# Three modulation vectors: sums over the k tiles elementwise on VectorE, only the sum over partitions on TensorE

## The chip, the cores and the metric

The kernel runs on one core of one Trainium2 chip. The metric is the device time of one execution in microseconds (us). The time before is the median of three runs.

## What is computed

One layer of a hybrid network over 640 tokens (128 of a context, 512 latent ones) of width 1024, all in float32: a SwiGLU block (FFN1), a mixer of two branches (a delta rule and windowed attention), a second SwiGLU block (FFN2) and a last norm. Nine modulation vectors of width 1024 scale, shift and gate these blocks, each for two conditions (the context's and the latents'). They come from one product of a vector with a 1024 x 9216 matrix, and this product is what the change is about:

```python
mod_p = (jax.nn.silu(c_ctx) @ ada_w[l] + ada_b[l])[None, None, :]
mod_s = (jax.nn.silu(c) @ ada_w[l] + ada_b[l])[:, None, :]
sh1p, sc1p, g1p, sh2p, sc2p, g2p, sh3p, sc3p, g3p = jnp.split(mod_p, N_MOD, axis=-1)
...
xp = ffn_sublayer(xp, norm_ffn1[l], sh1p, sc1p, g1p, ffn1_w13[l], ffn1_w2[l])
...
xp = ffn_sublayer(xp, norm_ffn2[l], sh3p, sc3p, g3p, ffn2_w13[l], ffn2_w2[l])
```

Vectors 0 and 1 are needed before FFN1 starts, 2 at its first residual, 3 to 5 in the mixer, and 6 to 8 (sh3, sc3, g3) in FFN2.

## The kernel before

The program is written as one stream and each engine keeps its own queue, in the order that a scheduler gave the instructions at build time. A queue is worked off in order: an instruction that waits holds up all behind it.

FFN1 (`ffn`, lines 480 to 528) goes through the 22 column blocks f of the hidden width in six rounds (ROUNDS: f = 0 to 2, 3 to 6, 7 to 10, 11 to 13, 14 to 17, 18 to 21). In a round it first makes the gated hidden blocks, then multiplies them by w2 and adds the result to the residual x (the w2 round: 8 column blocks d, `gated_add`, line 455). For f < 3 the two products are made directly; from f = 3 on `product_pair` (lines 570 to 613) makes both with seven products of a quarter size, whose weights are first combined on POOL (lines 580 to 583, tiles `ss`). Every weight tile is split into a high and a low part, the high part on ScalarE (line 127, tiles `wh` and `sh`) and the rest on DVE (line 128, `wl` and `sl`), and each product is three matmuls. `nraw` = 3 buffers hold raw weights, `nsh` = 6 hold each of `sh` and `sl` in FFN1; a pair uses five. FFN2 is the same code with `nsh` = 5 and without modulation.

Modulation vectors 2 to 8 are made in between (`modulation`, lines 266 to 301, called through `between` of line 1525). A vector takes four steps. A step loads two raw tiles of 128 x 1024 (line 273, tiles `araw`, a ring of two buffers) and multiplies each on TensorE by the 32 columns wide stationary tile `s32` (line 277): four matmuls for a raw tile, one for each 256 columns, each into its own 32 partitions of a PSUM tile, so that they sit on four column groups of the array. Both tiles of a step add up in PSUM; DVE adds the step's result to `modr` (lines 286 and 288). After the fourth step two transposes (line 292) and one addition (line 293) bring the vector into place. `between` does one step after each f (two for f = 0 and 1), and one each after d = 3 and d = 7 of each w2 round but the last. Tiles of PSUM are the ring `aux` of four and `big` of two.

Line numbers are those of the kernel before; behind line 265 those of the kernel after are higher by 4 to 51.

Of the kernel before, what the change touches and what calls it, by code (L numbers as in the profile page):

```python
# [10 lines left out]
F32 = mybir.dt.float32  # L11
# [4 lines left out]
ALU = mybir.AluOpType  # L16
# [3 lines left out]
P = 128  # L20
D = 1024
# [77 lines left out]
class Net:  # L99
# [147 lines left out]
    def vectors(self):  # L247
        nc = self.nc
        c = self.const
        ps = self.aux_tile()  # L250
        nc.tensor.transpose(ps[:, 0:16], self.crows, self.ident[0:16, 0:16])
        sT = self.tile(c, [P, 16], F32, "sT")
        nc.scalar.activation(sT, ps[:, 0:16], AF.Silu)
        self.s32 = self.tile(c, [P, KD, 32], F32, "s32")
        for v in range(2):
            nc.vector.tensor_copy(
                self.s32.rearrange("p k (r v) -> p v k r", v=2)[:, v],
                sT[:, v * 8 : v * 8 + 8].unsqueeze(2).to_broadcast([P, KD, 16]),
            )
        ps = self.aux_tile()  # L260
        nc.tensor.transpose(ps[:, 0:105], self.vrows[0:105], self.ident[0:105, 0:105])
        self.vecT = self.tile(c, [P, 105], F32, "vecT")
        nc.vector.tensor_copy(self.vecT, ps[:, 0:105])
        self.mod = self.tile(c, [P, 9, KD, 2], F32, "mod")

    def modulation(self, m):


        nc, a = self.nc, self.a
        r = self.tile(self.small, [P, 256], F32, "modr", 2)  # L270
        for k in range(KD):
            raw = self.tile(self.apool, [P, D], F32, "araw", 2)
            nc.sync.dma_start(raw, a["ada_w"][0, k * P : (k + 1) * P, m * D : (m + 1) * D])
            if k % 2 == 0:
                ps = self.aux_tile()[:, 0:256]
            for g in range(4):
                nc.tensor.matmul(  # L277
                    ps[32 * g : 32 * g + 32],
                    lhsT=self.s32[:, k, :],
                    rhs=raw[:, g * 256 : (g + 1) * 256],  # L280
                    start=(k % 2 == 0),
                    stop=(k % 2 == 1),
                )
            if k % 2:
                if k == 1:
                    nc.vector.tensor_copy(r, ps)
                else:
                    nc.vector.tensor_tensor(r, r, ps, op=ALU.add)
                yield
        p2 = self.aux_tile()  # L290
        for h in range(2):
            nc.tensor.transpose(p2[:, h * P : (h + 1) * P], r[:, h * P : (h + 1) * P], self.ident)
        nc.vector.tensor_tensor(
            self.mod[:, m].rearrange("p (g h) v -> p g h v", h=2),
            p2[:, 0:256].rearrange("p (h g r) -> p g h r", h=2, g=4)[:, :, :, 0:2],
            self.vecT[:, m * 8 : m * 8 + 8]
            .rearrange("p (g h) -> p g h", h=2)
            .unsqueeze(3)
            .to_broadcast([P, 4, 2, 2]),
            op=ALU.add,  # L300
        )

    def modulation_part(self, m0, d0, nd):

# [1121 lines left out]
    def build(self):  # L1426
        nc, a, tc = self.nc, self.a, self.tc
# [10 lines left out]
        with (  # L1438
# [9 lines left out]
            with (  # L1448
                pool("x1") as xpool,
            ):  # L1450
                self.setup()
                xall = self.tile(xpool, [P, KD, 2, HT], F32, "x")
                X = [xall[:, d] for d in range(KD)]
                self.apool = xpool
                ss = self.tile(self.const, [P, NCH], F32, "ss1")
                with pool("ada0", side="right") as ada, ExitStack() as inner:
                    with pool("in1", side="right") as self.phase:
                        self.load_input(xall, ss)
                        r = self.token_rstd(ss)
                        self.vectors()  # L1460
                    self.phase = ada
                    A1 = self.tile(self.const, [P, KD, 2], F32, "A1")
                    hs = self.operand_tiles(KD)
                    rb = []
                    for cuts in (((0, 0, P), (1, 0, P), (2, 0, HD)), ((2, HD, HD), (3, 0, P), (4, 0, P))):
                        o, columns = 0, []
                        for t, t0, n in cuts:
                            columns.append((r[:, t : t + 1], t0, n, o))
                            o += n
                        rb.append(self.half_rows(columns))  # L1470
                    xp = inner.enter_context(pool("xn", side="right"))
                    xn = [self.tile(xp, [P, 2, HT], F32, "xn", KD) for _ in range(KD)]

                    def scaled(d):
                        for h in range(2):
                            nc.vector.tensor_tensor(xn[d][:, h], X[d][:, h], rb[h], op=ALU.mult)

                    def first_steps(d0, after=None):
                        with self.tc.issue_after(after.ins) if after else ExitStack():
                            for ps, w in zip(first, ws):  # L1480
                                for d in (d0, d0 + 1):
                                    self.accumulate_step(ps, w, hs, d, 0, (0, 1))

                    for d in range(4):
                        scaled(d)
                    self.modulation_part(0, 0, 4)
                    mark = self.scale_columns(1, 72, A1, 0, 4)
                    pa = self.tile(self.big, [P, 2, 512], F32, "big", 2)
                    first = [[pa[:, h, 0:HT] for h in range(2)], [self.aux_tile()[:, 0:HT] for _ in range(2)]]
                    ws = []  # L1490
                    for d in range(4):
                        if d < 2:
                            ws.append(self.wcols(a["ffn1_w13"][0], (0, D_FF)[d]))
                        self.modulated_first(hs, xn, A1, 0, d)
                    first_steps(0)
                    with self.tc.issue_after(mark.ins):
                        for d in range(4, KD):
                            scaled(d)
                    last = self.modulation_part(0, 4, 2)
                    self.scale_columns(1, 72, A1, 4, 2)  # L1500
                    first_steps(2, last)
                    for d in (4, 5):
                        self.modulated_first(hs, xn, A1, 0, d)
                    last = self.modulation_part(0, 6, 2)
                    self.scale_columns(1, 72, A1, 6, 2)
                    first_steps(4, last)
                    for d in (6, 7):
                        self.modulated_first(hs, xn, A1, 0, d)
                    first_steps(6)
                with pool("g1", side="right") as self.phase:  # L1510
                    gates = {m: self.tile(self.const, [P, KD, 2], F32, f"gate{m}") for m in (2, 5, 8)}

                    def rest():
                        for m in range(2, 9):
                            yield from self.modulation(m)
                            if m in gates:
                                nc.vector.tensor_scalar(gates[m], self.mod[:, m], 0.5, None, op0=ALU.mult)
                        self.scale_columns(4, 80, A2)
                        self.scale_columns(7, 88, A3)
                        self.constants_late()  # L1520

                    A2, A3 = (self.tile(self.const, [P, KD, 2], F32, tag) for tag in ("A2", "A3"))
                    steps = rest()

                    def between(n):
                        for _ in range(n):
                            next(steps, None)

                    last = self.ffn(hs, X, gates[2], a["ffn1_w13"][0], a["ffn1_w2"][0], self.phase, between=between, first=first)
                    hs = self.next_operands(last, X, A2, 3)  # L1530
                    xd = dram([KD, P, T], "xd")
                    for d in range(KD):
                        nc.sync.dma_start(xd[d], flat(X[d]))


            with ExitStack() as right:
# [8 lines left out]
                with pool("mixt") as tmp, pool("attn") as at:  # L1545
# [29 lines left out]
                rest = [  # L1575
                    lambda off=off, chain=chain: list(chain(self.product(self.wcols(a["w_in"][0], off), hs)))
                    for off, chain in zs[2:]
                ]
# [78 lines left out]
```

## Time and profile before

| | |
|---|---|
| median of three runs | 1578.33 us (1575.17 to 1578.99) |
| the profiled execution | 1579.08 us |
| its span in the profile | 1577.4 us |
| mean granted clock of TensorE | 0.989 of full speed |
| TensorE busy | 1537.0 us |
| VectorE busy | 1091.9 us |
| ScalarE busy | 657.7 us |
| GpSimd busy | 293.6 us |

The profile is one execution. Busy times of an engine are what its instructions took, not what the kernel would gain without them. PE is TensorE's matmuls, PEld its weight loads, DVE is VectorE, ACT is ScalarE, POOL is GpSimd and SP the queue that issues nearly all DMAs. A TensorE row's duration is modelled and rows overlap, so the price of a group of matmuls is read from starts: when the next product starts, less when it would have started. FFN1 lies at about 45 to 430 us, FFN2 at about 1290 to 1575 us.

### The profile page before, as it was taken

What the parts mean: (1) busy time and instruction counts of PE and PEld (TensorE: products, weight loads), DVE (VectorE), ACT (ScalarE), POOL (GpSimd) and SP (SyncE); (2) the same over time, 40 slices, a digit from 0 to 9 for tenths busy, and PEclk for the clock granted to TensorE, in tenths of its full rate; (3) what the DMA queues carried; (4) which work ended last, traced back from release to release, by engine and by line L of the source; (5) the groups of instructions that cost most, each with busy time, mean ns of one, the idle gap of its engine ahead of it and who ended that gap; (6) DMA issues with size and microseconds to landing.
All of it is one profiled execution on the core that took longest, in us unless ns stands there. A gap on an engine that the chain in (4) does not pass through costs nothing.

```text
span 1577.4 us, 28409 instructions
## 1 busy us (share of the span) xinstructions
PE 1537.0 (97%) x11210; PEld 1458.9 (92%) x11210; DVE 1091.9 (69%) x2309; ACT 657.7 (42%) x1214; POOL 293.6 (19%) x240
## 2 busy tenths in 40 slices
PE   6999999999999899999999999999999999999998
PEld 4889999989999798788999999999899999999997
DVE  5877575658576758976765655765698776677676
ACT  4434232324243546564455544323353333334244
POOL 1022221222220110100321122000014141241410
PEclk8999999999999999999999999999999999999999
DMA  9654354445325341214533323445022313223122
GB/s 304 206 170 160 129 173 146 134 146 170 94 80 137 93 129 44 66 41 126 177 111 98 103 80 123 152 140 164 24 75 73 116 57 109 68 68 107 55 81 67
DMA packets 219119, 181.15 MB, mean 115 GB/s; under 512 B 16032, under 2 KB 194397, under 8 KB 218987
## 3 DMA queue, kind: packets, MB, share of 16 engines
q1 hardware_dynamic: 218731, 179.29, 37.2%
q8 instruction: 88, 1.44, 0.4%
q14 instruction: 44, 0.36, 0.1%
q0 software_dynamic: 256, 0.06, 0.0%
HBM read 161.59 MB, written 16.42 MB: 113 GB/s over the span
## 4 chain that ended last, share of the span: by engine, by line
PE 84%; DVE 7%; DMA 3%; ACT 2%; issue 2%; POOL 1%; SPq 0%; DVEq 0%; POOLq 0%; ACTq 0%
PE big L173 31%; PE aux L203 21%; PE aux L173 10%; PE aux L160 9%; PE big L203 8%; DMA wraw<-ffn_w 2%; DVE wl L128 1%; PE aux L277 1%; DVE x L455 1%; PE aux L157 1%; DVE sl L128 1%; ACT wh L127 1%; DVE cacc L870 1%; PE aux L317 1%; POOL ss L580 1%
## 5 line engine op out<-in xcount | busy, mean ns | idle before, releaser
L127 ACT CAST wh<-wraw 128x1024 fp32r<-128x1024 f32 (+1 forms) x147 | 150.6, 1027 | 270.0 <-PE big L173 89.9
L128 DVE TENSOR_TENSOR wl<-wraw,wh 128x1024 fp32r<-128x1024 f32 (+1 forms) x147 | 183.0, 1247 | 84.1 <-ACT wh L127 80.9
L173 PE MATMUL big<-hh,wh 128*128 128x320 f32 x768 | 192.9, 322 | 8.7 <-ACT hh L351 3.3
L173 PE MATMUL big<-hl,wh 128*128 128x320 f32 x768 | 192.3, 321 | 0.6 <-DVE hl L420 0.5
L173 PE MATMUL big<-hh,wl 128*128 128x320 f32 x768 | 188.1, 318 | 0.5 <-DVE wl L128 0.4
L580 POOL TENSOR_TENSOR ss<-wraw 128x512 f32<-128x512 f32 x38 | 51.2, 1349 | 725.3 <-DMA wraw<-ffn_w 648.6
L127 ACT CAST sh<-ss 128x512 fp32r<-128x512 f32 x152 | 92.7, 620 | 186.1 <-POOL ss L581 89.2
L128 DVE TENSOR_TENSOR sl<-ss,sh 128x512 fp32r<-128x512 f32 x152 | 133.2, 884 | 44.6 <-ACT sh L127 43.8
L173 PEld LDWEIGHTS big<-hh,wh 128*128 128x128 f32 x768 | 131.1, 191 | 15.1 <-ACT hh L351 5.5
L203 PE MATMUL aux<-th,sh 128*128 128x320 f32 x456 | 141.7, 311 | 2.2 <-DVE x L455 2.2
L203 PE MATMUL aux<-tl,sh 128*128 128x320 f32 x456 | 141.5, 310 | 0.0
L203 PE MATMUL aux<-th,sl 128*128 128x320 f32 x456 | 141.4, 310 | 0.0
L173 PEld LDWEIGHTS big<-hl,wh 128*128 128x128 f32 x768 | 131.3, 191 | 6.6 <-DVE hl L420 3.3
L173 PEld LDWEIGHTS big<-hh,wl 128*128 128x128 f32 x768 | 131.9, 191 | 3.3 <-issue 2.2
L455 DVE SCALAR_TENSOR_TENSOR x<-big,gate,x 128x128 f32<-128x128 f32 (+2 forms) x181 | 67.5, 424 | 36.4 <-PE big L173 36.1
L203 PEld LDWEIGHTS aux<-th,sh 128*128 128x128 f32 x456 | 86.2, 189 | 2.7 <-DVE x L455 2.7
L173 PE MATMUL big<-gh,wh 128*128 128x320 f32 x352 | 88.5, 313 | 0.0
L173 PE MATMUL big<-gl,wh 128*128 128x320 f32 x352 | 87.7, 310 | 0.0
L173 PE MATMUL big<-gh,wl 128*128 128x320 f32 x352 | 87.1, 309 | 0.0
L203 PEld LDWEIGHTS aux<-tl,sh 128*128 128x128 f32 x456 | 86.2, 189 | 0.0
L203 PEld LDWEIGHTS aux<-th,sl 128*128 128x128 f32 x456 | 86.2, 189 | 0.0
L1066 DVE TENSOR_TENSOR P<-aux,lv 128x512 f16<-128x512 f32 x70 | 48.2, 689 | 46.8 <-PE aux L160 46.8
(378 smaller groups left out, 3919.4 us busy)
## 6 DMA issues: line engine op xcount, KB each, us to landing
wraw<-ffn_w SPq DMA_DIRECT2D x116, 512.0 KB, 4.0
araw<-ada_w SPq DMA_DIRECT2D x64, 512.0 KB, 5.7
wraw<-w_in SPq DMA_DIRECT2D x35, 512.0 KB, 4.0
wraw<-ffn_w SPq DMA_DIRECT2D x16, 384.0 KB, 3.3
gd<-stage SPq DMA_DIRECT2D x16, 320.0 KB, 2.7
araw<-ada_w SPq DMA_DIRECT2D x16, 256.0 KB, 6.0
wraw<-w_out SPq DMA_DIRECT2D x8, 512.0 KB, 4.2
xd<-x SPq DMA_DIRECT2D x8, 320.0 KB, 2.2
```

The source lines that it names most:

```text
L127: nc.scalar.copy(hi, raw)
L128: nc.vector.tensor_sub(lo, raw, hi.bitcast(F32))
L157: self.marks.append(self.nc.tensor.transpose(*args))
L160: self.marks.append(self.nc.tensor.matmul(*args, **kw))
L173: self.nc.tensor.matmul(ps[h], lhsT=wt[:, k, c0 : c0 + P], rhs=xt[:, h, :], start=(k == 0 and j == 0), stop=(k == len(xs) - 1 and j == 2),)
L203: nc.tensor.matmul(ps, lhsT=wt[:, k * P : (k + 1) * P], rhs=xt, start=(k == 0 and j == 0), stop=(k == n - 1 and j == 2),)
L277: nc.tensor.matmul(ps[32 * g : 32 * g + 32], lhsT=self.s32[:, k, :], rhs=raw[:, g * 256 : (g + 1) * 256], start=(k % 2 == 0), stop=(k % 2 ...
L317: last = nc.tensor.matmul(ps[32 * j : 32 * j + 32], lhsT=self.s32[:, 2 * q + k, :], rhs=raw[:, k, m, :], start=(q == 0), stop=(q == 3),)
L455: nc.vector.scalar_tensor_tensor(X[:, h, cols], ps[:, cols], gate[:, d, v : v + 1], X[:, h, cols], op0=ALU.mult, op1=ALU.add)
L580: nc.gpsimd.tensor_tensor(f[0], b[:, :n], b[:, n:], op=ALU.add)
L870: nc.vector.scalar_tensor_tensor(acc, buf[:, t : t + n], w, acc, op0=ALU.mult, op1=ALU.add)
L1066: mark = nc.vector.tensor_tensor(P16, p1, mask, op=ALU.mult)
```

## The change

For vectors 6, 7 and 8 `modulation_sums` takes the place of the four steps. Half a vector (512 columns) at a time, it loads the matrix in four pieces of 128 x 2 x 512 (the same bytes in all); for each piece four DVE operations multiply both k tiles by the two conditions' scalars and add them up in `macc`. After the fourth piece the stationary tile `pick` (ones in every second column) sums each `macc` over the partitions: four matmuls of 256 columns for a half, two column groups with two matmuls each. What follows (transposes, addition of the bias) is as before, in a function of its own. The sums are a generator beside that of the steps: whenever `between` does one step, it now also does one piece of a sum, from f = 2 on. Both draw raw tiles from the ring `araw` of two. `nsh` goes from 6 to 5 in FFN1, and `constants_late` follows vector 5, not 8.

```diff
--- before.py
+++ after.py
@@ -262,6 +262,10 @@
         self.vecT = self.tile(c, [P, 105], F32, "vecT")
         nc.vector.tensor_copy(self.vecT, ps[:, 0:105])
         self.mod = self.tile(c, [P, 9, KD, 2], F32, "mod")
+        self.pick = self.tile(c, [P, 2, 32], F32, "pick")
+        nc.gpsimd.memset(self.pick, 0.0)
+        for v in range(2):
+            nc.gpsimd.memset(self.pick[:, v].rearrange("p (r v) -> p v r", v=2)[:, v], 1.0)
 
     def modulation(self, m):
 
@@ -287,6 +291,10 @@
                 else:
                     nc.vector.tensor_tensor(r, r, ps, op=ALU.add)
                 yield
+        self.modulation_vector(m, r)
+
+    def modulation_vector(self, m, r):
+        nc = self.nc
         p2 = self.aux_tile()
         for h in range(2):
             nc.tensor.transpose(p2[:, h * P : (h + 1) * P], r[:, h * P : (h + 1) * P], self.ident)
@@ -299,6 +307,40 @@
             .to_broadcast([P, 4, 2, 2]),
             op=ALU.add,
         )
+
+    def modulation_sums(self, m):
+
+
+        nc, a = self.nc, self.a
+        r = self.tile(self.small, [P, 256], F32, "modr", 2)
+        for half in range(2):
+            acc = self.tile(self.phase, [P, 2, 512], F32, "macc", 1)
+            for q in range(4):
+                raw = self.tile(self.apool, [P, 2, 512], F32, "araw", 2)
+                src = a["ada_w"][0, q * 256 : (q + 1) * 256, m * D + half * 512 : m * D + (half + 1) * 512]
+                nc.sync.dma_start(raw, src.rearrange("(k p) f -> p k f", p=P))
+                for k in range(2):
+                    for v in range(2):
+                        e = nc.vector
+                        s = self.s32[:, 2 * q + k, v : v + 1]
+                        if q == 0 and k == 0:
+                            e.tensor_scalar(acc[:, v], raw[:, k], s, None, op0=ALU.mult)
+                        else:
+                            e.scalar_tensor_tensor(acc[:, v], raw[:, k], s, acc[:, v], op0=ALU.mult, op1=ALU.add)
+                yield
+            ps = self.aux_tile()[:, 0:256]
+            for g in (2 * half, 2 * half + 1):
+                for v in range(2):
+                    nc.tensor.matmul(
+                        ps[32 * g : 32 * g + 32],
+                        lhsT=self.pick[:, v],
+                        rhs=acc[:, v, (g % 2) * 256 : (g % 2 + 1) * 256],
+                        start=(v == 0),
+                        stop=(v == 1),
+                    )
+            rows = slice(64 * half, 64 * half + 64)
+            nc.vector.tensor_copy(r[rows], ps[rows])
+        self.modulation_vector(m, r)
 
     def modulation_part(self, m0, d0, nd):
 
@@ -1511,21 +1553,30 @@
                     gates = {m: self.tile(self.const, [P, KD, 2], F32, f"gate{m}") for m in (2, 5, 8)}
 
                     def rest():
-                        for m in range(2, 9):
+                        for m in range(2, 6):
                             yield from self.modulation(m)
                             if m in gates:
                                 nc.vector.tensor_scalar(gates[m], self.mod[:, m], 0.5, None, op0=ALU.mult)
                         self.scale_columns(4, 80, A2)
+                        self.constants_late()
+
+                    def rest_sums():
+                        for m in range(6, 9):
+                            yield from self.modulation_sums(m)
+                            if m in gates:
+                                nc.vector.tensor_scalar(gates[m], self.mod[:, m], 0.5, None, op0=ALU.mult)
                         self.scale_columns(7, 88, A3)
-                        self.constants_late()
 
                     A2, A3 = (self.tile(self.const, [P, KD, 2], F32, tag) for tag in ("A2", "A3"))
-                    steps = rest()
+                    steps, sums = rest(), rest_sums()
 
                     def between(n):
                         for _ in range(n):
                             next(steps, None)
-
+                        if n == 1:
+                            next(sums, None)
+
+                    self.nsh = 5
                     last = self.ffn(hs, X, gates[2], a["ffn1_w13"][0], a["ffn1_w2"][0], self.phase, between=between, first=first)
                     hs = self.next_operands(last, X, A2, 3)
                     xd = dram([KD, P, T], "xd")
```

The SP queue, which issues the loads, around the pairs f = 3 and 4 (araw: raw tiles of the modulation; wraw: raw weights), before:

```order
L273 DMA araw_1238<-ada_w 128x1024
L273 DMA araw_1245<-ada_w 128x1024
L115 DMA wraw_1447<-ffn_w 128x8x128
L115 DMA wraw_1608<-ffn_w 128x8x128
L115 DMA wraw_1610<-ffn_w 128x8x128
L273 DMA araw_1428<-ada_w 128x1024
L273 DMA araw_1435<-ada_w 128x1024
L115 DMA wraw_1766<-ffn_w 128x8x128
L115 DMA wraw_1768<-ffn_w 128x8x128
L273 DMA araw_1591<-ada_w 128x1024
```

and now:

```order
L321 DMA araw_1148<-ada_w 128x2x512
L277 DMA araw_1256<-ada_w 128x1024
L115 DMA wraw_1477<-ffn_w 128x8x128
L277 DMA araw_1263<-ada_w 128x1024
L115 DMA wraw_1651<-ffn_w 128x8x128
L321 DMA araw_1270<-ada_w 128x2x512
L277 DMA araw_1452<-ada_w 128x1024
L115 DMA wraw_1653<-ffn_w 128x8x128
L277 DMA araw_1459<-ada_w 128x1024
L115 DMA wraw_1815<-ffn_w 128x8x128
L321 DMA araw_1466<-ada_w 128x2x512
```

The pieces of the sums (128x2x512) stand between the steps' two tiles and the weights. A step's second tile takes the buffer that the piece before it used.

The DVE queue at the end of the first w2 round, up to the first product of the pair f = 3 (line 596, u), before:

```order
L128 TENSOR_TENSOR wl_1458<-wraw_1445,wh_1457 128x1024
L128 TENSOR_TENSOR sl_1462<-ss_1450,sh_1461 128x512
L455 SCALAR_TENSOR_TENSOR x_92<-big_1193,gate_111_571,x_92 128x320
L455 SCALAR_TENSOR_TENSOR x_92<-big_1193,gate_111_571,x_92 128x128
L455 SCALAR_TENSOR_TENSOR x_92<-big_1193,gate_111_571,x_92 128x192
L455 SCALAR_TENSOR_TENSOR x_92<-aux_1215,gate_111_571,x_92 128x128
L455 SCALAR_TENSOR_TENSOR x_92<-aux_1216,gate_111_571,x_92 128x320
L455 SCALAR_TENSOR_TENSOR x_92<-aux_1215,gate_111_571,x_92 128x192
L288 TENSOR_TENSOR modr_1005<-modr_1005,aux_1240 128x256
L128 TENSOR_TENSOR wl_1621<-wraw_1608,wh_1620 128x1024
L596 TENSOR_TENSOR u_1323<-s_1254,aux_1338 128x320
```

and now:

```order
L497 SCALAR_TENSOR_TENSOR x_92<-big_1211,gate_112_575,x_92 128x320
L497 SCALAR_TENSOR_TENSOR x_92<-big_1211,gate_112_575,x_92 128x128
L497 SCALAR_TENSOR_TENSOR x_92<-big_1211,gate_112_575,x_92 128x192
L128 TENSOR_TENSOR sl_1344<-wraw_1313,sh_1343 128x512
L128 TENSOR_TENSOR wl_1488<-wraw_1475,wh_1487 128x1024
L497 SCALAR_TENSOR_TENSOR x_92<-aux_1234,gate_112_575,x_92 128x320
L497 SCALAR_TENSOR_TENSOR x_92<-aux_1233,gate_112_575,x_92 128x128
L497 SCALAR_TENSOR_TENSOR x_92<-aux_1233,gate_112_575,x_92 128x192
L292 TENSOR_TENSOR modr_1009<-modr_1009,aux_1258 128x256
L128 TENSOR_TENSOR wl_1664<-wraw_1651,wh_1663 128x1024
L329 SCALAR_TENSOR_TENSOR macc_1025<-araw_1270,s_32_199,macc_1025 128x512 x4
L638 TENSOR_TENSOR u_1347<-s_1278,aux_1362 128x320
```

The sl of the pair f = 4 (the row sl_1462<-ss_1450 of before) no longer stands ahead of the x updates; a group of four new operations stands behind the last wl, ahead of u.

PE where the first half of vector 6 is summed over partitions, behind a step:

```order
L281 MATMUL aux_1623<-araw_1621,s_32_199 32x256 x4
L281 MATMUL aux_1623<-araw_1628,s_32_199 32x256 x4
L334 MATMUL aux_1635<-macc_1025,pick_207 32x256 x4
L203 MATMUL aux_1688<-hh_213,wh_1663 128x320
```

The pick group follows a step's two groups directly; before, the products of the next pair came there.

## Rows read from the trace of the kernel before

**Rows 1.** Page, parts 1 and 4: busy times; chain by engine.

```profile
PE 1537.0 (97%) x11210; PEld 1458.9 (92%) x11210; DVE 1091.9 (69%) x2309; ACT 657.7 (42%) x1214; POOL 293.6 (19%) x240
...
PE 84%; DVE 7%; DMA 3%; ACT 2%; issue 2%; POOL 1%; SPq 0%; DVEq 0%; POOLq 0%; ACTq 0%
```

**Rows 2.** Groups by line: count | busy us, mean ns | idle before.

```profile
L277 PE MATMUL aux<-araw,s 128*32 128x256 f32 x448 | 30.4, 385 | 1.4 <-DVE x L455 1.1 <-DMA araw<-ada_w 0.3
```

**Rows 3.** Timeline (start us, us, instruction): PE around one step.

```profile
109.75 0.46 PE L173 MATMUL aux<-gh,wl 128*128 128x320 f32 x2
110.13 1.07 PE L277 MATMUL aux<-araw,s 128*32 128x256 f32 x16
...
111.13 0.41 PE L203 MATMUL aux<-hh,wh 128*128 128x320 f32 x1
...
111.38 0.31 PE L203 MATMUL aux<-hl,wh 128*128 128x320 f32 x1
...
213.88 1.07 PE L277 MATMUL aux<-araw,s 128*32 128x256 f32 x16
```

**Rows 4.** Timeline, PE around half a step.

```profile
55.15 0.31 PE L173 MATMUL big<-hh,wh 128*128 128x320 f32 x1
55.39 0.64 PE L277 MATMUL aux<-araw,s 128*32 128x256 f32 x8
55.96 0.41 PE L173 MATMUL big<-hh,wh 128*128 128x320 f32 x1
```

**Rows 5.** Round ends: a stretch's busy times; timeline with [idle <-releaser].

```profile
116.60:119.90 3.30, 3.30 (x15) 3.30 (x14) 1.39 (x3) 0.62 (x1) 1.38 (x1) 0.50 1.03 363
...
112.24 1.11 DVE L128 TENSOR_TENSOR sl<-ss,sh 128x512 fp32r<-128x512 f32 x1 [3.66 <-ACT sh L127]
...
115.17 0.41 PE L203 MATMUL aux<-th,sh 128*128 128x320 f32 x1 [2.01 <-DVE x L455]
...
116.65 0.47 PE L203 MATMUL aux<-th,sh 128*128 128x320 f32 x1
...
119.85 0.34 PE L203 MATMUL aux<-th,sh 128*128 128x320 f32 x1
...
201.38 0.38 PE L203 MATMUL aux<-hh,wh 128*128 128x320 f32 x1 [1.31 <-DVE x L455]
...
347.72 1.12 DVE L128 TENSOR_TENSOR sl<-ss,sh 128x512 fp32r<-128x512 f32 x1 [5.82 <-ACT sh L127]
...
350.65 1.07 PE L277 MATMUL aux<-araw,s 128*32 128x256 f32 x16 [1.09 <-DVE x L455]
```

**Rows 6.** Groups by line in FFN2 (1290 to 1575 us): last column is idle.

```profile
L203 PE MATMUL aux<-th,sh 128*128 128x320 f32 x157 | 48.5, 309 | 0.0
```

**Rows 7.** Timeline of DVE, POOL and SP in the pair that follows 213.88.

```profile
214.57 0.82 SPq L273 DMA_DIRECT2D araw<-ada_w  x2
214.72 0.68 DVE L128 TENSOR_TENSOR sl<-ss,sh 128x512 fp32r<-128x512 f32 x1
...
218.74 1.29 POOL L580 TENSOR_TENSOR ss<-wraw 128x512 f32<-128x512 f32 x1 [7.02 <-DMA wraw<-ffn_w]
...
219.20 1.39 DVE L128 TENSOR_TENSOR sl<-ss,sh 128x512 fp32r<-128x512 f32 x1
...
220.51 0.47 DVE L599 TENSOR_TENSOR s<-u,aux 128x320 f32<-128x320 f32 x1
...
220.72 1.29 POOL L581 TENSOR_TENSOR ss<-ss,wraw 128x512 f32<-128x512 f32 x1 [0.68 <-POOL ss L580]
```

**Rows 8.** Two pairs: PE, PEld, DVE, ACT, POOL busy; PEclk, DMA, GB/s.

```profile
213.90:227.40 13.50, 13.50 (x103) 12.72 (x102) 11.32 (x17) 6.06 (x10) 5.16 (x4) 1.00 0.44 148
227.40:240.90 13.50, 13.50 (x101) 12.72 (x100) 10.39 (x18) 6.80 (x11) 0.00 (x0) 1.00 0.57 189
```

**Rows 9.** DMA, 60 to 430 us: count, KB, us to landing.

```profile
araw<-ada_w SPq DMA_DIRECT2D x50, 512.0 KB, 5.6
wraw<-ffn_w SPq DMA_DIRECT2D x46, 512.0 KB, 4.3
```

## The prediction, made before the changed kernel was run

> **What bounds the kernel now.** I read the page first. PE is busy for 97% of the span and makes up 84% of the chain that ended last, while VectorE (DVE) is busy for 69% [rows 1]. So a microsecond taken from PE is a microsecond of time, unless PE then waits for someone. The granted clock is 0.989 of full speed on the mean of the span. Next I looked at what the changed lines cost PE. The groups by line give the 28 modulation steps of line 277 as 448 matmul records, 16 to a step [rows 2]. Their busy time is no price, because records overlap; the timeline gives it [rows 3]. The row at 109.75 holds two matmuls 0.15 us apart, so the next would start at 110.04. Instead the step's 16 records run, the next product starts at 111.13, and its second matmul comes 0.25 us later, not 0.15: a step costs (111.13 − 110.04) + 0.10 = **1.19 us**. A step of half the records [rows 4]: due at 55.30, next at 55.96, and the same 0.10 behind it: 0.76 us. So one set of four records on four column groups costs (1.19 − 0.76) / 2 = 0.215 us, and a group 0.33 us besides.
>
> Then I looked for what else PE loses in FFN1, which is where the change lies. After 100 us it waits for the x update three times, always at the end of a round: 2.01, 1.31 and 1.09 us [rows 5]. In the first and third the x updates stood in DVE's queue behind an sl of the next but one pair, which waited for ScalarE and POOL (DVE idle for 3.66 and 5.82 us); the second I could not put down to one such row. After the first wait the granted clock was 0.50, the lower of the two levels (1.2 GHz): the 12 matmuls from 116.65 to 119.85 stand 0.267 us apart, against 0.147 at the upper level, 1.4 us more [rows 5]. FFN2 runs the same code with five sh/sl buffers and no modulation: there the group that waited first here has no idle time [rows 6].
>
> **The change part by part.** *Off PE:* vectors 6, 7 and 8 lose four steps each: 12 × 1.19 = **−14.3 us**. Their transposes stay.
>
> *Onto PE:* six pick groups of four matmuls, eight records, on two column groups only. Priced by the set: 0.33 + 4 × 0.215 = 1.19 us if they run two at a time, 0.33 + 8 × 0.215 = 2.05 us if one at a time. The program writes both vectors of one column group one after the other, so neighbours share a group and I take 1.5 us, a little under the middle: 6 × 1.5 = **+9.0 us**, bounds 7.1 and 12.3. So more than half of the gain on PE goes back to PE.
>
> *Onto DVE:* 96 operations of 128x512. The nearest row is the sl of that shape, which also reads two SBUF tensors: 0.68 us when POOL is quiet, 1.39 us when it meets a POOL ss [rows 7]. Four come together, so a group takes 2.7 us; in all 96 × 0.68 = 65 us over some 300 us. Six fewer additions and copies of `modr`, each smaller than such an operation, are left out. What covers this? In a stretch of one product pair (13.5 us) DVE is busy 11.32 and 10.39 us [rows 8], so 2.2 to 3.1 us are free and 2.7 are wanted: the cover just about holds, with nothing over. Fifteen of the 24 groups lie in pairs; a lag of 0 to 0.6 us in each is 0 to 9 us. I take **+3 us**, because the w2 rounds between let DVE catch up. Behind a group that waits for its load stand, in the order shown ahead, the s and u of the same pair. Before, s came 6.6 us after the step (220.51 − 213.88) [rows 3, 7]; now the group can end up to 9.0 us after it (0.7 + 5.6 + 2.7, from the ring below). PE waits for such an operation only when it comes round to that bank of the four again, in the next pair, 13.5 us after the step: covered by 4.5 us, and without the cover 2.4 us a pair.
>
> One behaviour speaks against the change: the sl at 219.20 starts while the ss of 218.74 runs, and ends 0.56 us after it; the next ss starts only when that sl is done [rows 7]. Two operations that each read two SBUF tensors here ran one after the other, so a group that meets POOL lasts longer; the third rival has that price. The Trainium skill, "SBUF — State Buffer", section "SBUF: two separate sides", says that VectorE with two SBUF inputs and a GpSimd operation that reads SBUF take a shared port pair by an exclusive lock, and the later one is blocked fully. This trace agrees; by that rule alone, at every group, the time would be the third rival's, and by the quiet rows alone the forecast's.
>
> *The ring of raw tiles:* the loads of the sums use the same two buffers as the steps, and one sum runs with each step from f = 2 on. The buffer of a step's first tile is free at once; a sum's load takes it; and the next step's second tile can be loaded only when the four new DVE operations are done (the SP rows ahead show the order). From the rows: issue 0.7 us after the step (213.88, load issued at 214.57) [rows 3, 7], landing 4.3 us as a lone weight load of the same 512 KB has, up to the 5.6 us that modulation loads have [rows 9], group 2.7, landing again: 0.7 + 4.3 + 2.7 + 4.3 = 12.0 us, or 14.6, against the 13.5 us between two steps. Bounds 0 and 1.1 us a step; of the sixteen steps five lie at f < 3 and four in w2 rounds, which leaves 7 in pairs, 0 to 8 us. I take **+2 us**, nearer to the lone load since the pair of loads is now split. In the w2 rounds steps are farther apart than 15 us, so nothing there. Weight loads queue behind the waiting load in SP; three wraw buffers cover them, so nothing, and without that cover the same 0 to 1.1 us for each of the seven.
>
> *Buffers sh and sl, six to five:* the sl that was made two pairs ahead now stands behind the x updates (the DVE rows ahead show it for the first round end). The first and third wait go with the lower clock after the first: 2.0 + 1.1 + 1.4 = **−4.5 us**, bounds 0 and −5.8 (all three). Since [rows 6] shows five buffers without a wait, I take these two; at the second round end a group of new operations stands close by, so I leave that wait. The earlier constants, three memsets on POOL and the smaller loads lie before or beside, at nothing: PE does not wait for them in any row.
>
> **Sum:** −14.3 + 9.0 + 3 + 2 − 4.5 = −4.8 us. Against the profiled execution's 1579.08 us that is 1574.3; the median of the runs is 0.75 us lower, so **1573.5 us**. Below, all times are on the median's scale.
>
> **The rivals.** *Everything hides.* The pick groups run two at a time (7.1), DVE and ring cost nothing, all three waits go: −14.3 + 7.1 − 5.8 = −13.0, 1565.3 us. For it: PE waits only 0.3 us for these loads today [rows 2] and FFN2 shows no wait. Against it: DVE's thin cover, and pick matmuls that share a column group with their neighbour.
>
> *The gain is given back on PE and DVE.* Pick groups one at a time (12.3), the round-end waits stay in other clothes (0), lag +3: −14.3 + 12.3 + 3 = +1, 1579.3 us. For it: the sets of a step, which come back to the same column groups, stand 0.2 us apart and don't overlap, and a new operation waiting for its load can stand ahead of the x updates just as the sl did.
>
> *The ring through DVE becomes the bound: slower.* If the new operations meet POOL, a group takes 4 × 1.39 = 5.6 us. Then the ring takes 0.7 + 4.3 + 5.6 + 4.3 = 14.9 us with the short landing and 17.5 with the long, 1.4 to 4.0 over 13.5: seven steps × 2.7 = 19 us of PE waiting. The eight pairs after them have DVE over its 13.5 us by up to 0.6 (5 us). With −14.3 + 9.0 − 4.5 that is +14.2, 1592.5 us; half of the 24 us gives 1580.5. If groups met POOL only in every other pair it would be that. It decides where a group passes 13.5 − 0.7 − 2 × 4.3 = 4.2 us. For it: POOL works for 5.16 of a pair's 13.5 us where it works [rows 8]. Against it: in the other pairs POOL does nothing, and the groups stand behind the wl, early in a pair.
>
> **How the numbers follow.** About 0.3% (4.7 us) is what a measurement of this kernel can tell from no change, so 1573.6 and 1583.1 are the borders. Forecast 0.44, all hidden 0.17, given back 0.19, ring 0.20. The forecast lies on the border, its own range (1568 to 1579) half on each side: faster 0.23 + 0.17 + 0.01 from the second rival = 0.41; same 0.21 + 0.14 = 0.35; slower 0.20 from the ring and 0.04 from the second rival, 0.24. The range leaves out the upper half of the ring's case and the best of the hidden one: 1564 to 1588.
>
> **What would show it.** Right: 16 steps with 16 records each, pick groups 1.2 to 2.1 us from the matmul before to the one after; no wait for x at the first and third round end; DVE 1092 + 60 = 1150 us busy; new groups mostly below 3 us. Wrong: PE idle before the second half of a step, released by the araw load (the ring); groups of 5 us beside ss operations; waits for x behind the new operations; or, in the other direction, PE shorter by over 10 us with nothing in return.

## The result and the profile after

The changed kernel takes **1586.89 us** (median of 6 runs, 1583.21 to 1592.05); the kernel before, on the same chips, 1576.53 us. The ratio is 1.0057, with a 95% interval of 1.0041 to 1.0073: slower by about 10 us, where 5 us less were forecast. The profiled execution took 1588.96 us, its span is 1587.2 us.

Busy times and the chain, on the page of the kernel after:

```profile
PE 1535.0 (97%) x11066; PEld 1457.3 (92%) x11066; DVE 1169.4 (74%) x2399; ACT 655.9 (41%) x1214; POOL 302.5 (19%) x243
...
PE 77%; DVE 11%; DMA 5%; issue 3%; ACT 2%; POOL 1%; SPq 0%; DVEq 0%; POOLq 0%; ACTq 0%
```

Against [rows 1], PE has hardly less to do, DVE 77.5 us more, and PE's share of the chain went from 84 to 77%: DVE and DMA took it over. Next, whom PE waited for in FFN1. First the waits of the kernel before (60 to 435 us; us in total, times, longest), then those after (60 to 445 us):

```profile
PE aux L203 <- DVE x L455: 3.5, 3, 2.0
PE aux L277 <- DVE x L455: 1.1, 1, 1.1
PE aux L277 <- DMA araw<-ada_w: 0.3, 1, 0.3
```

```profile
PE aux L281 <- DMA araw<-ada_w: 6.6, 5, 2.6
PE big L173 <- DVE gl L547: 3.0, 1, 3.0
PE aux L203 <- DVE x L497: 2.5, 2, 1.5
PE aux L203 <- ACT gh L546: 0.9, 1, 0.9
PE aux L203 <- DVE modr L292: 0.7, 2, 0.4
```

4.9 us of waiting became 13.7 in these lines, 6.6 of it for raw tiles and the rest for what DVE, or ScalarE behind it, makes late. FFN1 doesn't end with these stretches, as the 430 us given ahead of the prediction would have it: its last round runs on to about 516 us before and 527 after, and that will matter below. The longest wait for a raw tile, on the timeline of the kernel after:

```profile
139.70 2.74 DVE L329 SCALAR_TENSOR_TENSOR macc<-araw,s,macc 128x512 f32<-128x512 f32 x4
142.46 0.34 SPq L277 DMA_DIRECT2D araw<-ada_w  x1
142.88 0.64 PE L281 MATMUL aux<-araw,s 128*32 128x256 f32 x8
146.12 0.64 PE L281 MATMUL aux<-araw,s 128*32 128x256 f32 x8 [2.60 <-DMA araw<-ada_w]
```

This is the ring as the prediction has it: the group of four ends at 142.44, the step's second tile is issued at 142.46, and the second half of the step, whose first half ran at 142.88, starts at 146.12. The longest wait for DVE:

```profile
337.67 1.62 POOL L622 TENSOR_TENSOR ss<-wraw 128x512 f32<-128x512 f32 x1 [26.04 <-DMA wraw<-ffn_w]
338.05 1.58 DVE L655 TENSOR_TENSOR s<-s,u 128x320 f32<-128x320 f32 x1
...
339.56 1.75 DVE L329 SCALAR_TENSOR_TENSOR macc<-araw,s,macc 128x512 f32<-128x512 f32 x1
...
341.23 3.03 DVE L547 TENSOR_TENSOR gl<-s,gh 128x320 fp32r<-128x320 f32 x2
...
342.83 0.63 PE L173 MATMUL big<-gl,wh 128*128 128x320 f32 x1 [3.01 <-DVE gl L547]
343.26 0.47 PE L173 MATMUL big<-gh,wl 128*128 128x320 f32 x1
343.53 0.47 PE L173 MATMUL big<-gh,wh 128*128 128x320 f32 x1
```

At the end of a round the operations of a sum, the last of a pair and POOL's ss meet. The s, macc and gl that meet an ss here last 1.5 to 1.75 us each; s and gl alone take 0.48. PE waits 3.01 us for gl, and behind the wait its matmuls stand 0.27 us apart, the spacing of the lower clock [rows 5]. No step took part in that wait, and PE waited for no raw tile there: the steps had ended at 253 us.

The pick groups, where the forecast took 1.5 us each:

```profile
322.50 0.31 PE L203 MATMUL aux<-hh,sl 128*128 128x320 f32 x1
322.74 1.06 PE L334 MATMUL aux<-macc,pick 128*32 128x256 f32 x8
323.73 0.42 PE L203 MATMUL big<-hh,wh 128*128 128x320 f32 x1
323.99 0.32 PE L203 MATMUL big<-hl,wh 128*128 128x320 f32 x1
```

The next product was due at 322.65 and came at 323.73, with another 0.11 behind it: 1.19 us, the same as a step and the lower bound. Three of the other five groups cost 1.15 to 1.19 us; one stood behind a wait for x, one ran at the lower clock. So the PE side came out as well as it could: −14.3 + 6 × 1.19 = −7.2 us.

### The profile page after: what moved, and what is told of

Read it like the earlier page. It is cut to its first block, busy times and chain, and to the rows that moved or that the text cites. A ratio compares the mean times of both kernels' runs of the same rounds, so it can differ in the third digit from the quotient of the medians.

```text
span 1587.2 us, 28223 instructions
## 1 busy us (share of the span) xinstructions
PE 1535.0 (97%) x11066; PEld 1457.3 (92%) x11066; DVE 1169.4 (74%) x2399; ACT 655.9 (41%) x1214; POOL 302.5 (19%) x243
## 4 chain that ended last, share of the span: by engine, by line
PE 77%; DVE 11%; DMA 5%; issue 3%; ACT 2%; POOL 1%; SPq 0%; DVEq 0%; POOLq 0%; ACTq 0%
PE big L173 32%; PE aux L203 16%; PE aux L173 10%; PE aux L160 9%; PE big L203 6%; DMA araw<-ada_w 3%; DVE macc L329 2%; DMA wraw<-ffn_w 2%; DVE sl L128 1%; DVE wl L128 1%; ACT wh L127 1%; DVE x L497 1%; PE aux L157 1%; DVE cacc L912 1%; POOL ss L625 1%
```

## The experiments

The theories. **R**, the ring: a sum's piece holds one of two raw buffers until DVE is done, and PE waits. **D**, DVE: the 96 operations by themselves make late what PE needs from DVE, and their meetings with POOL add to it. **B**: five sh/sl buffers in place of six cost something of their own. All times are medians; a kernel is compared with the kernel before on the same chip (1577.4 to 1578.5 us in the rows of the table). Each kernel is scheduled anew, so the order of the queues differs from run to run; no run holds that order fixed.

| kernel | us | ratio to before, 95% |
|---|---|---|
| before_nsh5 | 1579.73 | 1.0014 (1.0002 to 1.0026) |
| loads_only | 1578.70 | 1.0008 (0.9995 to 1.0022) |
| dve_no_ring | 1591.92 | 1.0084 (1.0069 to 1.0099) |
| sums_last | 1589.15 | 1.0062 (1.0042 to 1.0082) |
| nsh5_held | **1573.28** | **0.9970 (0.9958 to 0.9981)** |
| before_held | 1577.91 | 0.9998 (0.9988 to 1.0007) |
| after_held | 1584.56 | 1.0039 (1.0024 to 1.0054) |
| w2_sums | 1581.31 | 1.0021 (1.0011 to 1.0031) |
| own_ring | 1605.44 | 1.0170 (1.0156 to 1.0184) |
| extra_two_inputs | 1594.10 | 1.0112 (1.0095 to 1.0130) |
| extra_half | 1583.18 | 1.0036 (1.0021 to 1.0051) |
| extra_one_input | 1580.82 | 1.0020 (1.0011 to 1.0030) |

### Five buffers alone (before_nsh5)

```diff
+                    self.nsh = 5
                     last = self.ffn(hs, X, gates[2], ...
```

> The kernel before with one thing changed: five sh/sl buffers in FFN1, all modulation still on PE. The account of the prediction (two of the three waits for the x update at round ends go): -4.5 us against before, some 1572. Theory B (the five buffers are themselves what costs, since nothing is made ahead of a round end): slower than before by 3 to 10 us. The ring theory R and the DVE theory D say nothing against -4.5; if it comes out within 1 us of before, the buffers are neutral and neither gave nor took anything in the change.

1579.73 us, 2 us slower than before, and yet the forecast was right about its place. The s of one and the same pair, the first of FFN1's last round, before and with five buffers:

```profile
446.06 0.82 DVE L607 TENSOR_TENSOR s<-s,big 128x640 f32<-128x640 f32 x1 [1.69 <-PE big L203]
```

```profile
441.76 0.82 DVE L607 TENSOR_TENSOR s<-s,big 128x640 f32<-128x640 f32 x1 [1.84 <-PE big L203]
```

4.3 us had been won there, and the waits for x at the round ends were gone. They were lost again 40 us later, still in FFN1's last round:

```profile
481.77 1.04 ACT L127 CAST wh<-wraw 128x1024 fp32r<-128x1024 f32 x1 [6.10 <-DMA wraw<-w_in]
...
483.25 0.73 ACT L608 ACTIVATE s<-s 128x640 f32<-128x640 f32 x1
...
485.05 1.17 PE L173 MATMUL big<-gh,wh 128*128 128x320 f32 x3 [3.28 <-ACT gh L504]
```

ScalarE's queue has the cast of the mixer's first weight ahead of the activation of FFN1's last pair, and stands there until w_in has landed; behind PE's wait the matmuls stand 0.27 us apart (488.14, 488.41), the spacing of the lower clock. Before, the order was the same (the cast at 481.11, the activation at 484.24), but PE came there late enough for the load.

### The cast held back (nsh5_held, before_held, after_held)

```diff
+            with self.tc.issue_after(self.hold.ins) if self.hold else ExitStack():
                 nc.scalar.copy(hi, raw)
...
-                    nc.scalar.copy(gh[:, h], s[:, h])
+                    self.pair_end = nc.scalar.copy(gh[:, h], s[:, h])
...
+        self.hold = self.pair_end
+        wk = self.wcols(w_in, OFF_KB)
+        self.hold = None
+        ps = self.product(wk, hs)
-        ps = self.product(self.wcols(w_in, OFF_KB), hs)
```

> The kernel before with five sh/sl buffers, and the ScalarE cast of the mixer's first weight (w_in, line 127) put behind the last gated block of FFN1. With five buffers alone FFN1 was 4.2 us shorter at 438 us, but 3.4 us of wait and a lower clock came at 485 us, where ScalarE stood at that cast until w_in had landed (481.77). If that is what gave the 4.2 us back: 4 to 6 us below before, 1571 to 1574. If the five buffers cost in another place: within 2 us of 1579.

> The kernel before with six sh/sl buffers, and only the cast of w_in held back behind the last gated block. In its trace nobody on PE waits at that place (470 to 500 us). If the held cast gains only what the five buffers had lost there, this is the same as before within 2 us, and the 5 us of the run with both are those of the round ends. If it is 3 us or more below before, the held cast alone is the gain.

> The change with nothing but the cast of w_in held back. The wait at 497 us in the change's trace (1.33 us from start to start, 1.2 above a normal one) goes: 1 to 2 us below 1586.9. If it is faster by 5 or more, a good part of the loss stood at the way into the mixer, and not in the modulation.

With five buffers and the held cast: 1573.28 us, 0.3% below before and 14 us below the change: the fastest kernel of the study. PE's waits in FFN1 (60 to 435 us) are down to this:

```profile
PE aux L278 <- DMA araw<-ada_w: 0.3, 1, 0.3
PE aux L204 <- ACT gh L505: 0.3, 1, 0.3
```

The held cast without the five buffers changes nothing (0.9998), so the 5 us are the round ends' waits. In the changed kernel it gives 2 us, with intervals that overlap. The cleanest price of the sums is therefore the difference of two kernels that differ in them and what belongs to them (their memsets and the earlier constants), after_held and nsh5_held: **+11.3 us**, although PE has 7.2 us less to do. Some 18 us are lost elsewhere. Most of it is seen in PE's waits: from 60 to 520 us they add up to 16.4 us in the changed kernel and to 2.2 in nsh5_held.

### The loads without DVE's work, and DVE's work without the ring (loads_only, dve_no_ring)

```diff
-                            e.scalar_tensor_tensor(acc[:, v], raw[:, k], s, acc[:, v], ...)
+                            e.scalar_tensor_tensor(acc[:, v, 0:8], raw[:, k, 0:8], s, acc[:, v, 0:8], ...)
...
+                for k in range(2):
+                    for v in range(2):
+                        if q or k:
+                            s = self.s32[:, 2 * q + k, v : v + 1]
+                            nc.vector.scalar_tensor_tensor(acc[:, v], self.still, s, acc[:, v], ...)
```

The first two lines are loads_only, which leaves out most columns of the sums; dve_no_ring has the rest too, with `still` a high part of FFN1's input.

> The change, but 84 of the 96 new DVE operations work on 8 columns in place of 512 (so the last three modulation vectors are not the reference's; the loads, the ring of two, the pick groups and all waits stay). Ring theory R and DVE theory D agree: a piece's buffer comes free as soon as its load has landed and DVE has its time back, so -14.3 + 7.0 on PE and no new wait: 1566 to 1571 us. Theory B, or a cost in the order of the loads alone: above 1576.

> As the run with the short operations, and beside those the 84 operations of 512 columns again, but reading an operand of FFN1 that is long there in place of the raw tile (the last three vectors are not the reference's). DVE has its full work, and no raw tile is held by it. Ring theory R: the waits of PE for raw tiles (6.6 us, with the lower clock behind them about 8) go, the time is near that of the short operations, at most 3 us above it. DVE theory D: 72 us of DVE work beside POOL is what costs; the waits for the x updates, gl and modr stay, and the time is 6 us or more above that of the short operations, 1576 to 1582.

loads_only takes 1578.70 us, 8 to 13 above what both theories gave it. Making 84 of the 96 operations short wins 8.2 us against the change. Its waits (60 to 445 us):

```profile
PE aux L281 <- DMA araw<-ada_w: 4.2, 4, 2.1
PE big L173 <- ACT gh L546: 2.7, 1, 2.7
PE aux L203 <- DVE u L654: 1.1, 1, 1.1
```

Against before_nsh5 the 7.2 us of PE show up as 1.0 only, so what is left of the sums costs 6 us, and more if the cast of w_in is counted: before_nsh5 waits 3.3 us there, loads_only 1.3. By the price above it is about 18 − 8 = 10 us (an estimate). But it isn't the price of the loads alone. DVE still spends 28.5 us on the sums, against 77.3 in the change, because short operations and those left long meet POOL too (1590 ns the longest), and it stands in wait for raw tiles:

```profile
L329 DVE SCALAR_TENSOR_TENSOR macc<-araw,s,macc 128x8 f32<-128x8 f32 x84 | 20.9, 307 | 10.6 <-DMA araw<-ada_w 10.6
L327 DVE TENSOR_SCALAR macc<-araw,s 128x512 f32<-128x512 f32 x12 | 7.6, 663 | 1.2 <-DMA araw<-ada_w 1.2
```

And the wait of 2.7 us is one of queue order: here ScalarE's cast of the next pair's sh, which waits for POOL, stands ahead of the last activation of the round; in nsh5_held that activation (321.85) comes before the casts (327.91).

```profile
328.78 0.62 ACT L127 CAST sh<-ss 128x512 fp32r<-128x512 f32 x1 [7.66 <-POOL ss L623]
329.31 0.73 ACT L650 ACTIVATE s<-s 128x640 f32<-128x640 f32 x1
```

So part of R holds: the shared ring shows with 4.2 us of waits for raw tiles even where DVE has less work. dve_no_ring takes 1591.92 us, 13.2 more (the short operations are still there beside the wide ones, 22.4 us of DVE), and its waits are DVE's and those of ScalarE behind it:

```profile
PE aux L203 <- DVE x L502: 4.8, 2, 2.6
PE aux L203 <- ACT gh L551: 4.3, 3, 2.0
PE big L173 <- ACT gh L551: 1.9, 1, 1.9
```

Raw tiles are waited for 0.7 us in all, where the change waits 6.6, and the kernel isn't faster for it, though the short operations count against it. With sums_last below, which waits for no raw tile and is as slow as the change, R as the main cause falls. That DVE catches up while PE waits for a raw tile, so that the two costs don't add, would explain it; it was not tested.

### The sums elsewhere (sums_last, w2_sums, own_ring)

```diff
 sums_last
+                            if next(steps, self) is self:
+                                next(sums, None)
+                                next(sums, None)
 w2_sums
-                            for m in range(2, 6):
+                            for m in range(2, 7):
...
+                        if n:
+                            for _ in range(n):
+                                next(steps, None)
+                        else:
+                            next(sums, None)
+                            next(sums, None)
...
-                        between(1)
+                        between(0)
 own_ring
-                raw = self.tile(self.apool, [P, 2, 512], F32, "araw", 2)
+                raw = self.tile(self.phase, [P, 2, 256], F32, "sraw", 1)
```

> The change, with the sums only after the last step: no step and no sum share the ring, and two pieces follow each call for the last 13 calls in place of one for 24. Ring theory R: no wait of PE for raw tiles, about -7 against before, 1568 to 1573. DVE theory D: eight operations (6 us) in each of the last pairs, which have 2 to 3 us free: at least 3 us of lag in each of some nine pairs, 1590 or more.

> Two vectors (7 and 8) in place of three by sums on DVE, and all 16 pieces in the w2 rounds 1 to 4 (four a round), none in a pair; steps only behind the f; five buffers and the cast held back as in the run beside it. Ring theory R: no step and no sum share the ring at one time, so 8 steps x 1.19 - 4 pick groups x 1.16 = -4.9 against the run with five buffers and the held cast. DVE theory D: a w2 round has 32 us and 19 us of DVE work, so four pieces (12 us) just fit; the x updates come late by up to one piece (3 us) at the end of a round: between -5 and +6 against that run.

> The whole change (three vectors, from f = 2 on), but the sums have a raw tile and a sum of their own, both of 256 columns (one buffer each, the same 4 KB), and two pieces follow each call; 192 operations of 256 columns in place of 96 of 512. No step waits for a buffer that a sum holds. Ring theory R: the waits for raw tiles (6.6 us and the clock behind them) go: 1578 to 1580 against 1586.9 with the shared ring. DVE theory D: DVE has its work and 96 more starts of an operation: no better than 1587.

None shares a buffer between a step and a sum that run together, and none is fast. sums_last: 1589.15 us, 16 above the range of R and just below D's bound of 1590; no wait for raw tiles worth naming, but DVE full in the stretch of the sums (PE, PEld, DVE, ACT, POOL busy of 55 us):

```profile
345.00:400.00 55.00, 46.02 (x297) 42.62 (x296) 54.78 (x77) 18.65 (x32) 22.76 (x14) 0.97 0.43 125
```

w2_sums, with 64 operations where DVE had most room and 8 × 1.19 − 4 × 1.19 = 4.8 us off PE, is 8.0 us above nsh5_held: 13 us for 64 operations. Both theories had given it less (R −4.9, D +6 at most). own_ring is the slowest, but it isn't a clean test of R: it has twelve pick groups, 0.96 us from the first matmul to the next product for four records as for eight, which makes some 6 us more on PE (an estimate), smaller and more operations, and DVE waits for its one raw buffer:

```profile
211.35 1.03 PE L334 MATMUL aux<-macc,pick 128*32 128x256 f32 x4
212.31 0.41 PE L203 MATMUL big<-hh,wh 128*128 128x320 f32 x1
```

```profile
L330 DVE SCALAR_TENSOR_TENSOR macc<-sraw,s,macc x168: 466/480/1525, 80.2 to 440.6; 128x256 f32<-128x256 f32 x168
...
  DMA sraw<-ada_w: 23.2, 13
```

### DVE's work alone (extra_two_inputs, extra_half, extra_one_input)

All three are nsh5_held with operations added that nobody needs, no load and no matmul changed:

```diff
+                        if n == 1 and len(self.extra) < 24:
+                            self.extra.append(0)
+                            for j in range(4):
+                                nc.vector.scalar_tensor_tensor(acc[:, j % 2], still, self.s32[:, 0, 0:1], acc[:, j % 2], ...)
 extra_half: range(2)
 extra_one_input
+                                nc.vector.tensor_reduce(acc[:, j : j + 1], still, ...)
```

> The kernel with five buffers and the held cast (1573.3), all modulation on PE, and beside it 96 operations of the sums' kind and size (128x512, two operands in SBUF, some 0.74 us), four at each of the 24 places where the change has a piece of a sum; they work on data of FFN1 into a tile that nobody reads. No load, no ring, no matmul is changed: only DVE's work. DVE theory D: it costs by itself what the change lost, 10 to 17 us, 1583 to 1590. If the operations are harmless where no loads hang on them: 1573 to 1576, and the loads' waiting in DVE's queue is what costs.

> The same with two operations at each place in place of four. If the cost is in proportion to the work: half of the other run's. If it sets in only where the free 2 to 3 us of a pair are used up: near zero, 1573 to 1576.

> The same as with four operations, but each a sum over 512 columns into one (one operand in SBUF, nearly the same duration). If DVE's time alone costs: as with two operands, within 3 us. If it is the meeting with POOL of operations with two SBUF operands: at least 5 us less than with two.

Above nsh5_held these stand by 20.8, 9.9 and 7.5 us (on another chip; the kernel before takes 1578.23 us there and 1578.45 here). The first is more than expected, and half the operations cost half: 48 operations show no free allowance in DVE's idle time that is used up first. (The scheduler also put them earlier and closer together than the sums, 78 to 298 us against 94 to 410.) The third run tells part of why. The operations' durations (ns, shortest, median, longest) with two operands in SBUF, and with one:

```profile
L1540 DVE SCALAR_TENSOR_TENSOR macc<-hh,s,macc x96: 733/741/1804, 78.2 to 298.0; 128x512 f32<-128x512 f32 x96
```

```profile
L1539 DVE TENSOR_REDUCE macc<-hh x96: 667/672/680, 78.2 to 260.4; 128x1 f32<-128x512 f32 x96
```

The same place in both, first with two operands, then with one:

```profile
138.38 1.63 POOL L581 TENSOR_TENSOR ss<-wraw 128x512 f32<-128x512 f32 x1 [6.66 <-DVE s L600]
138.78 1.78 DVE L1540 SCALAR_TENSOR_TENSOR macc<-hh,s,macc 128x512 f32<-128x512 f32 x1
...
143.33 1.78 DVE L1540 SCALAR_TENSOR_TENSOR macc<-hh,s,macc 128x512 f32<-128x512 f32 x1
...
149.12 0.60 PE L204 MATMUL aux<-th,sh 128*128 128x320 f32 x1 [4.31 <-ACT gh L505]
```

```profile
140.67 2.21 POOL L583 TENSOR_TENSOR ss<-wraw,wraw 128x512 f32<-128x512 f32 x1 [0.63 <-DVE sl L129]
141.65 0.67 DVE L1539 TENSOR_REDUCE macc<-hh 128x1 f32<-128x512 f32 x1
```

Not one of the 96 sums with a single operand in SBUF was held up, though 25 of them ran beside an ss; of the operations with two, 16 lasted over 1.7 us, 1804 ns the longest. The cost falls from 20.8 to 7.5 us, the operations' DVE time from 83.8 to 60.5. Some 16 × 1.04 = 17 us of that time is the meeting with POOL, and 96 × 0.07 = 7 the longer operation. So the meeting is the likely reason for most of the 13.3 us between the runs, though the two also differ in that operation's length, in what it writes and in where the scheduler put it; the 7.5 us are what the added DVE time costs where no added operation is held up.

The Trainium skill, "SBUF — State Buffer", section "Who interferes with whom", says that a VectorE operation with two operands in SBUF contends with a GpSimd operation that reads SBUF; the durations in these two kernels agree with it (up to 1804 ns with two operands, at most 680 in the sums with one).

## Why the prediction was wrong

*Off PE* held: the steps' 448 records became 256, and a step that nothing delays still costs 1.19 us.

*Onto PE*, +9.0: measured 7.1, the lower bound. The two matmuls on one column group follow each other, as was feared, but the two groups ran at the same time all the same.

*Onto DVE*, "+3, bounds 0 to 9": **this is the step that failed.** It compared the free part of a pair (2.2 to 3.1 us) with the work added (2.7) and took what fits to be free. The runs with added operations alone show 10 and 21 us for 48 and 96 of them, in proportion. In the change itself the width of 84 operations is worth 8.2 us (loads_only), near the upper bound, and with the ring, the loads and the short operations that loads_only still has it is 18 us against nsh5_held, where +3 and +2 were forecast. DVE's idle time in a pair lies in waits for PE's next result and for ScalarE, and its queue is in order, so an operation put elsewhere delays what stands behind it (the gl at 341.23 behind the macc at 339.56 shows it once; in general it is argued, not tested apart); and the mean price of an operation wasn't 0.68 us. The group of the 84 in the changed kernel:

```profile
L329 DVE SCALAR_TENSOR_TENSOR macc<-araw,s,macc 128x512 f32<-128x512 f32 x84 | 72.0, 901 | 6.5 <-DMA araw<-ada_w 6.5
```

901 ns on the mean, 744 in the median; 13 of the 84 lasted over 1.5 us. What they hold up (POOL's ss, then the s and gl that meet the later ss) is in none of these 72 us. The row that speaks for this, [rows 7], was read, and used only for a rival.

*The ring*, +2: mis-sized. The wait is there, 6.6 us (0.3 before), near the upper bound of 8, but only 4.3 of it lies in pairs (at 146.12 and 238.98); 1.9 us lie at the ends of w2 rounds (114.23 and 208.16), where the forecast had nothing. The term's first number was off: in the step shown the load is issued not 0.7 us after the step before, but 5.5 (134.06 behind a step at 128.55), because SP had a weight load ahead that waited for its own buffer. Only the reverse, weight loads behind a raw tile, had been thought of, at nothing. But the ring isn't what made most of the loss: without its waits the time didn't fall.

*Five buffers*, −4.5: right in size and place without the sums (4.3 us at the start of FFN1's last round, 5 us with the held cast), and wrong in the sum, because what is late next was not looked for in that last round: the cast that waits for w_in. By itself the edit came out at +2. In the changed kernel little of the gain shows: PE still waits 3.4 us for x (4.6 before) and 3.0 for gl at a round end, which is the second rival's "other clothes".

*The rivals.* The ring through DVE, given 0.20 at 1592.5 us, had the right sign and the meetings with POOL, but its sum came near by luck: it took 19 us of waits at the ring, where PE waited 6.6, and it let every operation meet POOL, where 13 of the 84 did so at their cost. For DVE itself it took 0.6 us a pair, although its own groups of 5.6 us in the busier pair of [rows 8] give 11.32 + 5.6 − 13.5 = 3.4. The price of the DVE queue that the runs show stood within reach there. That 1586.89 us still lies inside 1564 to 1588 is owed to this rival, which widened the range, and not to the forecast.

What stays open: how the 18 us divide between loads, queue order and DVE's work in the changed kernel. The width of 84 operations is worth 8.2 us; the other 10 (an estimate) hold waits for raw tiles, waits by queue order and 28.5 us of DVE work, and no run separates them.

## What to carry to other kernels

Idle time of an engine with an in-order queue is not in itself an allowance for new work: price the work by what stands behind it in that queue, and by whom it meets on another engine, not by the share that is free. When two engines contend operation by operation, look up in the trace which operations are lengthened beside the other engine: here a sum with one operand in SBUF was not, while one with two was. And when an edit gains at one place, look at the next wait along the chain, to the end of the stage and beyond: here 5 us hung on the place of one cast in ScalarE's queue.

## What was not expected of the hardware

Four matmuls of 32 columns, on two column groups in the order A A B B, took 1.19 us, as much as eight on four groups in the order A B C D twice; and two matmuls on one group (own_ring, 0.96 us from start to the next product) as much as four on two (322.74 to 323.73, 0.99). So the two groups overlapped though they weren't interleaved in the program. And the sum over 512 columns, one operand in SBUF, was never lengthened by POOL in 96 operations (667 to 680 ns), while macc, sl, s and gl, which have two, were. One tensor operand alone is no protection, though: the multiplications that start a sum (TENSOR_SCALAR, one raw tile and a scalar for each partition), 482 ns in the median of loads_only, lasted 1590 and 1566 ns where two of them met ss operations (from 262.37 us).
